# Layer 1's feed-forward part in one written order of block products and down products

## Chip, core and metric

The kernel runs on one core of one Trainium2 chip. A core has five engines with a queue each: TensorE (PE, with its weight loads shown as PEld), VectorE (DVE), ScalarE (ACT), GpSimd (POOL) and SyncE (SP), which here only issues DMAs. Each executes its queue in order and waits on semaphores for the others. The metric is device time in microseconds, the median of three runs.

## What is computed

A two-layer block over 1024 latent tokens of width 1024 and 256 context tokens. The change lies in the last part, the feed-forward of layer 1, which works on the latent tokens alone:

```python
x = x + g1 * o
h = _rms(x, norm2_g[i]) * (1.0 + sc2) + sh2
x = x + g2 * _swiglu(h, ffn_w_gate[i], ffn_w_up[i], ffn_w_down[i])

def _swiglu(h, wg, wu, wd):
    return (jax.nn.silu(h @ wg) * (h @ wu)) @ wd
```

The hidden width is 2816, which is 22 tiles of 128 (`NF = 22`). All values are 32-bit floats.

## The kernel before

**Precision.** A product of 32-bit floats is made of three matmuls: each operand is split into a rounded high part and a low part (the rest), and high by high, low by high and high by low are summed in PSUM (`mm3`, lines 74 to 76). The split of a weight tile is `parts_of` (lines 1236 to 1246): ScalarE casts to the high part (L1240), ScalarE copies that to a PSUM tile `pmisc` (L1244), and VectorE subtracts (L1245). With `G` as engine, Pool subtracts from SBUF directly. The ring for split weights has six places (`w_hi`, `w_lo`).

**Tiles of the feed-forward.** The tokens are done in two halves of 512 (`ci`). For each of 22 tiles (`f`) of the hidden width, gate and up together are a 2 x 2 block product, done as seven products of blocks instead of eight (`gate_up1`, with `product7`): each has 4 x 3 = 12 matmuls of 256 columns. Four raw weight blocks (b11, b12, b22, b21) of 128x512 are loaded by SP; four sums of them, t1 to t4, are made on Pool (L1328, L1329, L1343, L1347). The seven results are combined by VectorE (u2, u3, av, sg), with two Silu on ScalarE and two multiplications on VectorE (L1360, L1366), and the 512 values per partition of the tile's activation are split into `act_hi` (ScalarE, L1368) and `act_lo` (VectorE, L1369).

**Down.** Two tiles at a time are multiplied by w_down: eight down products (`down1`), each of 6 matmuls of 512 columns into one of three PSUM buffers `d_ps`, added into x by VectorE (L1394). The last eight of a half store x (L1396), issued from ScalarE's queue. The w_down weights are loaded by DMAs issued from Pool's queue (L1383) and split by ScalarE (L1384) and Pool (L1385).

**Norm and combine.** `norm1s` makes the normed activations of a half as a series of small steps, which other loops call for one at a time (`advance`). For the first half (`own0`) its steps run beside the output projection `out_proj1`; those of the second half (`own1`) begin beside the output projection too and go on with two steps per tile. The results of the second half are kept in DRAM (`h_d`) until the first half is done, then read back (`h_in`) and combined by `combine` into the 14 blocks `c_hi`, `c_lo` that the products read.

**Order of the work.** In this part the order in which each engine's queue is filled is the planner's: it takes the instructions as the program emits them and places them by its own estimates of cost. Other parts of the kernel fix the order of emission with `tc.manual_schedule`. In the program, a tile's seven products come one after the other, with the split of a product's weights just ahead of it (t1 and t2 of the first tile earlier), and after every second tile the eight down products of the pair before.

Of the kernel before, what the change touches and what calls it, by code (L numbers as in the profile page):

```python
# [16 lines left out]
P = 128  # L17
# [46 lines left out]
def build(tc, io):  # L64
# [1209 lines left out]
    def norm1s(ci, adder, done):  # L1274


        ts = slice(ci * 512, ci * 512 + 512)
        ss = wk.tile([P, 512], F32, name="nrm_ss")
        for i, k in enumerate(reversed(range(KT))):
            if i == 0:  # L1280
                S.activation(ss, x[:, k, ts], AF.Square)
            else:
                sq = wk.tile([P, 512], F32, name="nrm_sq", tag="t", bufs=4)
                S.activation(sq, x[:, k, ts], AF.Square)
                adder.tensor_tensor(ss, ss, sq, ALU.add)
            yield
        for r in norm_rstd(ss, 512, wk, ph):
            yield
        for i in range(4):
            both = []  # L1290
            for k in (i, i + 4):
                t = wk.tile([P, 512], F32, name="nrm_t", tag="t", bufs=4)
                V.scalar_tensor_tensor(t, x[:, k, ts], nA[3][:, k, 0:1], r, ALU.mult, ALU.mult)
                h = wk.tile([P, 512], F32, name="nrm_h", tag="wd", bufs=4)
                S.activation(h, t, AF.Identity, bias=vec(1, 3)[:, k, 0:1], scale=1.0)
                both.append(h)
                yield
            done(i, *both)
            yield
# [22 lines left out]
    def load_gate_up(f):  # L1322

        return [raw_half(io[w][1, f][:, i:i + 4]) for w, i in (("w_gate", 0), ("w_up", 0), ("w_up", 4), ("w_gate", 4))]

    def first_sums(b11, b12, b22):
        t1, t2 = (wk.tile([P, 4, P], F32, name=n, tag="t", bufs=4) for n in ("t1", "t2"))
        G.tensor_tensor(t1, b12, b11, ALU.subtract)  # L1328
        G.tensor_tensor(t2, b22, t1, ALU.subtract)  # L1329
        return t1, t2  # L1330

    def gate_up1(f, side=iter(()), raws=None):
        b11, b12, b22, b21 = raws[:4] if raws else load_gate_up(f)
        t1, t2 = raws[4:] if raws else first_sums(b11, b12, b22)
        t3, t4 = (wk.tile([P, 4, P], F32, name=n, tag="t", bufs=4) for n in ("t3", "t4"))
        p1, u2, u3, sg = (wk.tile([P, HT], F32, name=n) for n in ("p1", "u2", "u3", "sg"))
        av = wk.tile([P, 2, HT], F32, name="av", bufs=2)
        hi, lo = (wk.tile([P, 512], F32R, name=n, bufs=4) for n in ("act_hi", "act_lo"))
        w = parts_of(b11)
        ps = product7(w, 0)  # L1340
        S.copy(p1, ps)
        w = parts_of(t2)
        G.tensor_tensor(t3, b22, b12, ALU.subtract)  # L1343
        ps = product7(w, 4)
        V.tensor_tensor(u2, ps, p1, ALU.add)
        w = parts_of(t3)
        G.tensor_tensor(t4, t2, b21, ALU.subtract)  # L1347
        ps = product7(w, 5)
        V.tensor_tensor(u3, ps, u2, ALU.add)
        w = parts_of(t1)  # L1350
        ps = product7(w, 3)
        V.tensor_tensor(av[:, 1], ps, u3, ALU.add)
        V.tensor_tensor(u2, ps, u2, ALU.add)
        w = parts_of(t4)
        ps = product7(w, 2)
        V.tensor_tensor(u3, u3, ps, ALU.subtract)
        S.activation(u3, u3, AF.Silu)
        w = parts_of(b21)
        ps = product7(w, 1)
        V.tensor_tensor(av[:, 1], av[:, 1], u3, ALU.mult)  # L1360
        V.tensor_tensor(sg, ps, p1, ALU.add)
        S.activation(sg, sg, AF.Silu)
        w = parts_of(b22, G)
        ps = product7(w, 6)
        V.tensor_tensor(u2, ps, u2, ALU.add)
        V.tensor_tensor(av[:, 0], u2, sg, ALU.mult)  # L1366
        avf = av.rearrange("p a n -> p (a n)")
        S.copy(hi, avf)  # L1368
        V.tensor_tensor(lo, avf, fl(hi), ALU.subtract)  # L1369
        advance(side, 2)  # L1370
        return hi, lo
# [4 lines left out]
    h_d = tc.dram_tile([P, KT, 512], F32, name="h_d")  # L1376

    def down_weights1(f):

        w_in = w_room[f // 2 % 2]  # L1380
        for h in range(2):
            raw = wk.tile([P, 4, P], F32, name="wd_raw", tag="wd", bufs=4)
            G.dma_start(raw, io["w_down"][1, f][:, 4 * h:4 * h + 4])  # L1383
            S.copy(w_in[:, f % 2, h, 0], raw)  # L1384
            G.tensor_tensor(w_in[:, f % 2, h, 1], raw, fl(w_in[:, f % 2, h, 0]), ALU.subtract)  # L1385

    def down1(ci, fs, acts, last, amid=lambda dt: None):
        w_in = w_room[fs[0] // 2 % 2]
        ts = slice(ci * 512, ci * 512 + 512)
        for dt in range(KT):  # L1390
            ps = pd.tile([P, 512], F32, name="d_ps")
            for i in range(2):
                mm3(ps, w_in[:, i, dt // 4, 0, dt % 4], w_in[:, i, dt // 4, 1, dt % 4], *acts[i], i == 0, i == 1)
            V.scalar_tensor_tensor(x[:, dt, ts], ps, vec(1, 5)[:, dt, 0:1], x[:, dt, ts], ALU.mult, ALU.add)  # L1394
            if last:
                nc.scalar.dma_start(io["out"][:, dt, ts], x[:, dt, ts])  # L1396
            amid(dt)

    def keep(i, h0, h4):
        for k, h in ((i, h0), (i + 4, h4)):  # L1400
            nc.scalar.dma_start(h_d[:, k], h)

    own0 = norm1s(0, G, combine)
# [5 lines left out]
    own1 = norm1s(1, V, keep)  # L1409
    def first_tile():  # L1410
        raws = load_gate_up(0)
        return *raws, *first_sums(*raws[:3])

    ready = out_proj1(1, ready, own1, own0, then=first_tile)
    advance(own0, 99)
    for ci in range(2):
        acts = {}
        for f in range(NF):
            acts[f] = gate_up1(f, own1 if f else iter(()), ready if f + ci == 0 else None)
            down_weights1(f)  # L1420
            if f % 2 == 0 and 2 <= f < NF - 2:
                down1(ci, (f - 2, f - 1), [acts.pop(f - 2), acts.pop(f - 1)], False)

        h_in = []
        for i in range(4 if ci == 0 else 0):
            if i:
                h_in.append([raw_half(h_d[:, k]) for k in (i, i + 4)])
            else:
                h_in.append([wk.tile([P, 512], F32, name="h_in", tag=t) for t in ("nrm_ss", "nrm_r")])
                for h, k in zip(h_in[0], (0, 4)):  # L1430
                    nc.sync.dma_start(h, h_d[:, k])

        def amid(i):
            if h_in and i in (3, 7, 9, 12):
                combine(4 - len(h_in), *h_in.pop(0), tags=("t", "t"))

        for f in (NF - 4, NF - 2):
            down1(ci, (f, f + 1), [acts.pop(f), acts.pop(f + 1)], f == NF - 2,
                  lambda dt, f=f: amid(dt + (KT if f == NF - 2 else 0)))
# [113 lines left out]
```

## Time and profile before

| | us |
|---|---|
| median of three runs | 2944.4 |
| lowest and highest run | 2942.7, 2944.55 |
| the profiled execution | 2949.19 |
| its span on the core | 2947.4 |
| TensorE busy in the span | 2812.9 (95%) |
| VectorE, ScalarE, Pool busy | 1592.2, 1219.9, 799.0 |

The profile is one execution; its times are in microseconds from the start of the span, a duration in nanoseconds where it says "mean". A matmul's recorded time overlaps the next one's, so a busy TensorE can still lose time: the distance from one start to the next is what a matmul costs. In a row of the timeline, `[1.17 <-DVE x L1394]` says that the engine was idle 1.17 us before this instruction and that VectorE's instruction of line 1394 released it. In a row of groups, the figures after the bar are busy time, mean duration of one in ns, and the idle time ahead of them with what ended it. In a row of stretches stand the stretch, its length, busy time and count for each engine, the granted clock of TensorE as a share of full speed, and the DMA share and rate.

### The profile page before, as it was taken

What the parts mean: (1) busy time and instruction counts of PE and PEld (TensorE: products, weight loads), DVE (VectorE), ACT (ScalarE), POOL (GpSimd) and SP (SyncE); (2) the same over time, 40 slices, a digit from 0 to 9 for tenths busy, and PEclk for the clock granted to TensorE, in tenths of its full rate; (3) what the DMA queues carried; (4) which work ended last, traced back from release to release, by engine and by line L of the source; (5) the groups of instructions that cost most, each with busy time, mean ns of one, the idle gap of its engine ahead of it and who ended that gap; (6) DMA issues with size and microseconds to landing.
All of it is one profiled execution on the core that took longest, in us unless ns stands there. A gap on an engine that the chain in (4) does not pass through costs nothing. (4 is left out here: it accounts for less than half of the span.)

```text
span 2947.4 us, 44547 instructions
## 1 busy us (share of the span) xinstructions
PE 2812.9 (95%) x16874; PEld 2350.1 (80%) x16874; DVE 1592.2 (54%) x3144; ACT 1219.9 (41%) x2402; POOL 799.0 (27%) x870
## 2 busy tenths in 40 slices
PE   7989999999999999999989999999989899989999
PEld 5876768888888888888857778777768788888898
DVE  5775553633323333333575252566566777877776
ACT  4345552421111111111253231566447666666664
POOL 1122332000000000000130001455246666676662
PEclk9989999999999999999989999999999999999999
DMA  7236564211011110110124335876343322233231
GB/s 277 85 118 231 213 210 148 65 43 36 29 50 36 36 43 29 43 43 29 54 79 142 108 105 153 186 182 145 117 150 118 128 98 100 99 136 100 97 104 47
DMA packets 149349, 310.59 MB, mean 105 GB/s; under 512 B 13424, under 2 KB 71280, under 8 KB 142096
## 3 DMA queue, kind: packets, MB, share of 16 engines
q1 hardware_dynamic: 133664, 265.73, 28.9%
q0 software_dynamic: 8992, 31.40, 3.3%
q10 hardware_dynamic: 6480, 10.63, 1.0%
q8 instruction: 133, 2.18, 0.3%
q14 instruction: 80, 0.66, 0.1%
HBM read 264.58 MB, written 43.12 MB: 104 GB/s over the span
## 5 line engine op out<-in xcount | busy, mean ns | idle before, releaser
L74 PE MATMUL p_ps<-c_hi,w_hi 128*128 128x256 f32 x1232 | 344.6, 280 | 13.6 <-ACT w_hi L1240 4.6
L76 PE MATMUL p_ps<-c_hi,w_lo 128*128 128x256 f32 x1232 | 343.0, 279 | 4.5 <-DVE w_lo L1245 3.5
L75 PE MATMUL p_ps<-c_lo,w_hi 128*128 128x256 f32 x1232 | 342.7, 278 | 0.0
L810 POOL TENSOR_TENSOR nrm_ss<-nrm_ss,nrm_sq 128x512 f32<-128x512 f32 (+1 forms) x31 | 39.4, 1271 | 1012.9 <-PE d_ps L76 935.4
L775 ACT CAST w_hi<-w_raw 128x1024 fp32r<-128x1024 f32 x106 | 110.5, 1051 | 485.1 <-PE d_ps L75 270.4
L74 PEld LDWEIGHTS p_ps<-c_hi,w_hi 128*128 128x128 f32 x1232 | 233.7, 190 | 17.5 <-ACT w_hi L1240 6.6
L76 PEld LDWEIGHTS p_ps<-c_hi,w_lo 128*128 128x128 f32 x1232 | 233.5, 190 | 5.8 <-DVE w_lo L1245 4.5
L75 PEld LDWEIGHTS p_ps<-c_lo,w_hi 128*128 128x128 f32 x1232 | 233.6, 190 | 0.9
L580 POOL TENSOR_SCALAR pr<-pr,st 128x640 f32<-128x640 f32 (+2 forms) x208 | 156.9, 755 | 266.7 <-DVE st L579 176.8
L878 DVE SCALAR_TENSOR_TENSOR x<-d_ps,mod,x 128x512 f32<-128x512 f32 (+1 forms) x240 | 157.6, 661 | 125.2 <-PE d_ps L76 125.2
L776 DVE TENSOR_TENSOR w_lo<-w_raw,w_hi 128x1024 fp32r<-128x1024 f32 x102 | 124.1, 1224 | 184.0 <-ACT w_hi L775 181.6
L862 DVE TENSOR_TENSOR sg<-sg,u_ps 128x512 f32<-128x512 f32 (+1 forms) x66 | 39.6, 599 | 322.4 <-PE u_ps L76 322.4
L74 PE MATMUL d_ps<-act_hi,w_hi 128*128 128x512 f32 (+1 forms) x528 | 188.8, 358 | 3.5 <-DVE x L878 3.4
L75 PE MATMUL d_ps<-act_lo,w_hi 128*128 128x512 f32 (+1 forms) x528 | 188.7, 357 | 1.3 <-DVE act_lo L864 1.3
L75 PE MATMUL u_ps<-o_lo,w_hi 128*128 128x512 f32 (+1 forms) x528 | 189.3, 358 | 0.0
L76 PE MATMUL u_ps<-o_hi,w_lo 128*128 128x512 f32 (+1 forms) x528 | 189.1, 358 | 0.0
L74 PE MATMUL u_ps<-o_hi,w_hi 128*128 128x512 f32 (+1 forms) x528 | 189.0, 358 | 0.0
L76 PE MATMUL d_ps<-act_hi,w_lo 128*128 128x512 f32 (+1 forms) x528 | 188.9, 358 | 0.0
L74 PE MATMUL g_ps<-o_hi,w_hi 128*128 128x512 f32 (+1 forms) x528 | 188.2, 357 | 0.0
L75 PE MATMUL g_ps<-o_lo,w_hi 128*128 128x512 f32 (+1 forms) x528 | 188.2, 356 | 0.0
L76 PE MATMUL g_ps<-o_hi,w_lo 128*128 128x512 f32 (+1 forms) x528 | 188.2, 356 | 0.0
L574 ACT ACTIVATE pr<-sm,st 128x640 f32<-128x640 f32 (+4 forms) x208 | 162.9, 783 | 31.1 <-POOL sm L563 22.3
(329 smaller groups left out, 7494.6 us busy)
## 6 DMA issues: line engine op xcount, KB each, us to landing
ada_w<-ada_w SPq DMA_DIRECT2D x48, 1024.0 KB, 4.9
wd_raw<-w_down POOLq DMA_DIRECT2D x88, 256.0 KB, 2.9
w_raw<-w_gate SPq DMA_DIRECT2D x88, 256.0 KB, 2.6
w_raw<-w_up SPq DMA_DIRECT2D x88, 256.0 KB, 2.7
k<-k_d SPq DMA_DIRECT2D x28, 640.0 KB, 10.5
w_raw<-w_in SPq DMA_DIRECT2D x24, 512.0 KB, 4.0
w_raw<-w_gate SPq DMA_DIRECT2D x22, 512.0 KB, 3.5
w_raw<-w_up SPq DMA_DIRECT2D x22, 512.0 KB, 3.5
```

The costliest lines, as they stand in the source:

```text
L74: TE.matmul(out, lh, rh, start=first, stop=False)
L75: TE.matmul(out, lh, rl, start=False, stop=False)
L76: TE.matmul(out, ll, rh, start=False, stop=last)
L574: S.activation(self.pr[:, :n], self.sm[:, :n], AF.Exp, bias=st[:, 0:1], scale=-1.0, accum_out=st[:, 1:2])
L580: G.tensor_scalar(self.pr[:, :n], self.pr[:, :n], st[:, 3:4], 0.0, ALU.mult, ALU.add)
L775: S.copy(hi, raw)
L776: eng.tensor_tensor(lo, raw, fl(hi), ALU.subtract)
L810: adder(i).tensor_tensor(ss, ss, sq, ALU.add)
L862: V.tensor_tensor(sg[:, :n], sg[:, :n], u_ps[:, :n], ALU.mult)
L878: V.scalar_tensor_tensor(xs, self.shaped(ps[:, :n]), vec(l, 5)[:, dt, v:v + 1], xs, ALU.mult, ALU.add)
```

## The change

The whole part is emitted as one list of items: for each tile its seven products ("p"), after the third tile on also four down products ("d") of the pair before the last, and at the end of a half the last eight. A loop goes through the list inside `tc.manual_schedule`, so that TensorE, VectorE, ScalarE and Pool issue in the order of emission; SP's DMAs stay with the planner. Ahead of each item the loop emits the split of weights up to five products ahead (and at most seven items ahead), sums included. Steps that need a result of the item before (Silu, the multiplications, the split of the activation) are emitted one to three items later. In detail:

- `act_lo` is made on Pool instead of VectorE.
- The w_down loads are issued from SP instead of Pool, in the tile's fourth product; their split comes in the next tile.
- The second half's norm begins only in the second tile of the feed-forward, one step at every second product; its additions and multiplications are on Pool, with the scale moved into ScalarE's activation, its squares and its results in one buffer each (`nrm_r`, `nrm_ss`).
- Ahead of the first item, beside the last step of the output projection, five products' weights of the first tile are prepared instead of the two sums t1 and t2.
- `combine` for the second half stands at fixed places among the last twelve down products of the first half.

```diff
@@ -1271,7 +1271,7 @@
             advance(side, 3)
         return ready
-    def norm1s(ci, adder, done):
+    def norm1s(ci, done):
         ts = slice(ci * 512, ci * 512 + 512)
@@ -1280,23 +1280,31 @@
             if i == 0:
                 S.activation(ss, x[:, k, ts], AF.Square)
             else:
-                sq = wk.tile([P, 512], F32, name="nrm_sq", tag="t", bufs=4)
+                sq = wk.tile([P, 512], F32, name="nrm_sq", **(dict(tag="nrm_r") if ci else dict(tag="t", bufs=4)))
                 S.activation(sq, x[:, k, ts], AF.Square)
-                adder.tensor_tensor(ss, ss, sq, ALU.add)
+                G.tensor_tensor(ss, ss, sq, ALU.add)
             yield
         for r in norm_rstd(ss, 512, wk, ph):
             yield
         for i in range(4):
             both = []
             for k in (i, i + 4):
-                t = wk.tile([P, 512], F32, name="nrm_t", tag="t", bufs=4)
-                V.scalar_tensor_tensor(t, x[:, k, ts], nA[3][:, k, 0:1], r, ALU.mult, ALU.mult)
-                h = wk.tile([P, 512], F32, name="nrm_h", tag="wd", bufs=4)
-                S.activation(h, t, AF.Identity, bias=vec(1, 3)[:, k, 0:1], scale=1.0)
+                a, b = nA[3][:, k, 0:1], vec(1, 3)[:, k, 0:1]
+                if ci:
+                    h = wk.tile([P, 512], F32, name="nrm_h", tag="nrm_ss")
+                    G.tensor_tensor(h, x[:, k, ts], r, ALU.mult)
+                    S.activation(h, h, AF.Identity, bias=b, scale=a)
+                    nc.scalar.dma_start(h_d[:, k], h)
+                else:
+                    t = wk.tile([P, 512], F32, name="nrm_t", tag="t", bufs=4)
+                    V.scalar_tensor_tensor(t, x[:, k, ts], a, r, ALU.mult, ALU.mult)
+                    h = wk.tile([P, 512], F32, name="nrm_h", tag="wd", bufs=4)
+                    S.activation(h, t, AF.Identity, bias=b, scale=1.0)
                 both.append(h)
                 yield
-            done(i, *both)
-            yield
+            if not ci:
+                done(i, *both)
+                yield
     M1, M2 = slice(0, HT), slice(HT, 2 * HT)
@@ -1319,124 +1327,174 @@
             mm3(ps, w[0][:, k], w[1][:, k], c_hi[:, slot, k], c_lo[:, slot, k], k == 0, k == 3)
         return ps
-    def load_gate_up(f):
-
...
+    items = []
+    for ci in range(2):
+        for f in range(NF):
+            items += [("p", ci, f, s) for s in range(7)]
+            if f >= 2:
+                items += [("d", ci, f // 2 * 2 - 2, dt) for dt in range(f % 2 * 4, f % 2 * 4 + 4)]
+        items += [("d", ci, NF - 2, dt) for dt in range(KT)]
+    products = [(n, i) for n, i in enumerate(items) if i[0] == "p"]
+    LEAD_P, LEAD_I = 5, 7
+    tiles = {}
+    def load_tile(n):
+        if n < 2 * NF:
+            f = n % NF
+            tiles[n] = dict(b=[raw_half(io[w][1, f][:, i:i + 4])
+                               for w, i in (("w_gate", 0), ("w_up", 0), ("w_up", 4), ("w_gate", 4))], w={})
+    def prepare1(n, s):
+        if s == 0:
+            load_tile(n + 1)
+        d = tiles[n]
+        b11, b12, b22, b21 = d["b"]
+        def weight_sum(name, a, b):
+            d[name] = wk.tile([P, 4, P], F32, name=name, tag="t", bufs=4)
+            G.tensor_tensor(d[name], a, b, ALU.subtract)
+        if s == 0:
+            weight_sum("t1", b12, b11)
+            weight_sum("t2", b22, d["t1"])
+        elif s == 1:
+            weight_sum("t3", b22, b12)
+        elif s == 3:
+            weight_sum("t4", d["t2"], b21)
+        src = (b11, d["t2"], d.get("t3"), d["t1"], d.get("t4"), b21, b22)[s]
+        d["w"][s] = parts_of(src, G if s == 6 else V)
     w_room = [t.rearrange("p k n -> p (k n)").rearrange("p (f h t k n) -> p f h t k n", f=2, h=2, t=2, n=P)
               for t in h_out[1]]
     h_d = tc.dram_tile([P, KT, 512], F32, name="h_d")
-
-    def down_weights1(f):
-
-        w_in = w_room[f // 2 % 2]
+    down_raw = {}
+    def load_down(n):
         for h in range(2):
             raw = wk.tile([P, 4, P], F32, name="wd_raw", tag="wd", bufs=4)
-            G.dma_start(raw, io["w_down"][1, f][:, 4 * h:4 * h + 4])
-            S.copy(w_in[:, f % 2, h, 0], raw)
-            G.tensor_tensor(w_in[:, f % 2, h, 1], raw, fl(w_in[:, f % 2, h, 0]), ALU.subtract)
-
-    def down1(ci, fs, acts, last, amid=lambda dt: None):
-        w_in = w_room[fs[0] // 2 % 2]
+            nc.sync.dma_start(raw, io["w_down"][1, n % NF][:, 4 * h:4 * h + 4])
+            down_raw[n, h] = raw
+    def split_down(n, h):
+        f = n % NF
+        hi, lo = (w_room[f // 2 % 2][:, f % 2, h, t] for t in range(2))
+        raw = down_raw.pop((n, h))
+        S.copy(hi, raw)
+        G.tensor_tensor(lo, raw, fl(hi), ALU.subtract)
+    later = {}
+    def product(i, n, s):
+        d = tiles[n]
+        if s == 0:
+            for name in ("p1", "u2", "u3", "sg"):
+                d[name] = wk.tile([P, HT], F32, name=name)
+            d["av"] = wk.tile([P, 2, HT], F32, name="av", bufs=2)
+            d["act"] = [wk.tile([P, 512], F32R, name=m, bufs=4) for m in ("act_hi", "act_lo")]
+        p1, u2, u3, sg, av, (hi, lo) = (d[k] for k in ("p1", "u2", "u3", "sg", "av", "act"))
+        ps = product7(d["w"].pop(s), (0, 4, 5, 3, 2, 1, 6)[s])
+        def after(k, f):
+            later.setdefault(i + k, []).append(f)
+        if s == 0:
+            S.copy(p1, ps)
+        elif s == 1:
+            V.tensor_tensor(u2, ps, p1, ALU.add)
+        elif s == 2:
+            V.tensor_tensor(u3, ps, u2, ALU.add)
+        elif s == 3:
+            V.tensor_tensor(av[:, 1], ps, u3, ALU.add)
+            V.tensor_tensor(u2, ps, u2, ALU.add)
+        elif s == 4:
+            V.tensor_tensor(u3, u3, ps, ALU.subtract)
+            after(1, lambda: S.activation(u3, u3, AF.Silu))
+        elif s == 5:
+            V.tensor_tensor(sg, ps, p1, ALU.add)
+            after(1, lambda: S.activation(sg, sg, AF.Silu))
+            after(1, lambda: V.tensor_tensor(av[:, 1], av[:, 1], u3, ALU.mult))
+        else:
+            avf = av.rearrange("p a n -> p (a n)")
+            V.tensor_tensor(u2, ps, u2, ALU.add)
+            after(1, lambda: V.tensor_tensor(av[:, 0], u2, sg, ALU.mult))
+            after(2, lambda: S.copy(hi, avf))
+            after(3, lambda: G.tensor_tensor(lo, avf, fl(hi), ALU.subtract))
+    def down_product(ci, n, dt):
+        f = n % NF
+        w_in = w_room[f // 2 % 2]
         ts = slice(ci * 512, ci * 512 + 512)
-        for dt in range(KT):
-            ps = pd.tile([P, 512], F32, name="d_ps")
...
+        ps = pd.tile([P, 512], F32, name="d_ps")
+        for i in range(2):
+            mm3(ps, w_in[:, i, dt // 4, 0, dt % 4], w_in[:, i, dt // 4, 1, dt % 4], *tiles[n + i]["act"],
+                i == 0, i == 1)
+        V.scalar_tensor_tensor(x[:, dt, ts], ps, vec(1, 5)[:, dt, 0:1], x[:, dt, ts], ALU.mult, ALU.add)
+        if f == NF - 2:
+            nc.scalar.dma_start(io["out"][:, dt, ts], x[:, dt, ts])
+    own0 = norm1s(0, combine)
     ready = out_proj1(0, out_weights(KT - 1), own0, then=lambda: out_weights(KT - 1))
     pools.close(bg_cms[0])
     cc, cc_cm = pools.open("comb", side="right")
     c_hi = cc.tile([P, 7, 4, HT], F32R, name="c_hi")
     c_lo = cc.tile([P, 7, 4, HT], F32R, name="c_lo")
-    own1 = norm1s(1, V, keep)
+    own1 = norm1s(1, None)
     def first_tile():
-        raws = load_gate_up(0)
-        return *raws, *first_sums(*raws[:3])
-
-    ready = out_proj1(1, ready, own1, own0, then=first_tile)
+        load_tile(0)
+        for s in range(LEAD_P):
+            prepare1(0, s)
+    out_proj1(1, ready, iter(()), own0, then=first_tile)
     advance(own0, 99)
-    for ci in range(2):
-        acts = {}
...
+    done_p = LEAD_P
+    h_in = []
+    with tc.manual_schedule(engines={E.PE, E.DVE, E.Activation, E.Pool}):
+        now_p = 0
+        for i, (kind, ci, f, s) in enumerate(items):
+            n = ci * NF + f
+            while done_p < len(products) and done_p < now_p + LEAD_P + 1 and products[done_p][0] <= i + LEAD_I:
+                _, pc, pf, ps_ = products[done_p][1]
+                prepare1(pc * NF + pf, ps_)
+                done_p += 1
+            for step in later.pop(i, ()):
+                step()
+            if kind == "p":
+                product(i, n, s)
+                now_p += 1
+                if s == 3:
+                    load_down(n)
+                if f and s in (2, 5):
+                    split_down(n - 1, s // 5)
             else:
-                h_in.append([wk.tile([P, 512], F32, name="h_in", tag=t) for t in ("nrm_ss", "nrm_r")])
-                for h, k in zip(h_in[0], (0, 4)):
...
+                down_product(ci, n, s)
+                last = i + 12 >= len(items) or items[min(i + 12, len(items) - 1)][1] > ci
+                rest = sum(1 for it in items[i:i + 12] if it[0] == "d" and it[1] == ci) if last else 13
+                if last and rest in (12, 10):
+                    split_down(ci * NF + NF - 1, 0 if rest == 12 else 1)
+                if last and ci == 0 and rest in (11, 8, 5, 2):
+                    j = (11 - rest) // 3
+                    combine(j, *h_in[j], tags=("t", "t"))
+            if ci == 0 and kind == "p" and f and s % 2 == 0:
+                advance(own1, 1)
+            if ci == 0 and kind == "p" and f == NF - 1 and s == 6:
+                rooms = [dict(tag="nrm_ss"), dict(tag="nrm_r")], *([dict(tag="wd", bufs=4)] * 2,) * 3
+                for k, room in enumerate(rooms):
+                    h_in.append([raw_half(h_d[:, m]) if k in (1, 2) else wk.tile([P, 512], F32, name="h_in", **r)
+                                 for m, r in zip((k, k + 4), room)])
+                    if k in (0, 3):
+                        for h, m in zip(h_in[k], (k, k + 4)):
+                            nc.sync.dma_start(h, h_d[:, m])
+        for i in sorted(later):
+            for step in later[i]:
+                step()
     pools.close(ph_cm, pp_cm, pd_cm, wk_cm, ww_cm, wr_cm, xp_cm, cc_cm, bg_cms[1], cst_cm)
```

## What the change is predicted to do

> **What bounds the kernel now.** First the page's span, then layer 1's feed-forward part, which begins with the first product at 2204.3 us, in five stretches cut where a block of down products ends.
>
> ```profile
> span 2947.4 us, 44547 instructions
> ```
>
> The view by stretches, for the product tile p_ps and then for the down tile d_ps; columns: length, PE busy (matmuls), granted clock, DMA share, GB/s.
>
> ```profile
> 2204.30:2341.20 136.90, 76.02 (x588) 0.90 0.38 128
> 2341.20:2531.30 190.10, 115.30 (x1008) 1.00 0.30 100
> 2531.30:2638.50 107.20, 61.03 (x504) 0.98 0.36 123
> 2638.50:2892.40 253.90, 154.14 (x1344) 1.00 0.30 99
> 2892.40:2943.80 51.40, 28.74 (x252) 1.00 0.08 31
> ...
> 2204.30:2341.20 136.90, 40.45 (x145) 0.90 0.38 128
> 2341.20:2531.30 190.10, 69.68 (x289) 1.00 0.30 100
> 2531.30:2638.50 107.20, 35.22 (x145) 0.98 0.36 123
> 2638.50:2892.40 253.90, 92.84 (x385) 1.00 0.30 99
> 2892.40:2943.80 51.40, 22.79 (x98) 1.00 0.08 31
> ```
>
> A product is 12 matmuls, a down product 6 (one more at a cut is the neighbour's). So the stretches hold 49, 84, 42, 112, 21 products and 24, 48, 24, 64, 16 down products. The timeline gives what each costs when nothing waits:
>
> ```profile
> 2492.88 0.39 PE L75 MATMUL d_ps<-act_lo,h_lo 128*128 128x512 f32 x1
> ...
> 2499.41 0.39 PE L76 MATMUL d_ps<-act_hi,h_lo 128*128 128x512 f32 x1
> ...
> 2499.64 0.28 PE L74 MATMUL p_ps<-c_hi,w_hi 128*128 128x256 f32 x1
> ...
> 2504.75 0.28 PE L74 MATMUL p_ps<-c_hi,w_hi 128*128 128x256 f32 x1
> ```
>
> 28 down matmuls start in 6.53 us, so 1.40 us for a down product; 45 product matmuls in 5.11 us, so 1.363 us for a product. TensorE's need is 308 x 1.363 + 176 x 1.40 = 666 us of the 739.5. Lost by stretch: 136.9 - 100.4 = **36.5**, 190.1 - 181.7 = **8.4**, 107.2 - 90.9 = **16.3**, 253.9 - 242.3 = **11.6**, 51.4 - 51.0 = **0.4**: 73.2 us in all, the most that any order of these items can win here. Half lies in the first seven tiles. In the steady stretches 20 us are lost in 14 pairs of tiles, 1.4 us a pair, by one wait:
>
> ```profile
> 2488.87 1.30 POOL L1347 TENSOR_TENSOR t<-t,w_raw 128x512 f32<-128x512 f32 x1
> 2489.12 1.33 DVE L1366 TENSOR_TENSOR av<-u,sg 128x256 f32<-128x256 f32 x1
> 2490.37 0.67 DVE L1245 TENSOR_TENSOR w_lo<-w_raw,pmisc 128x512 fp32r<-128x512 f32 x1
> ...
> 2491.14 0.69 DVE L1369 TENSOR_TENSOR act_lo<-av,act_hi 128x512 fp32r<-128x512 f32 x1
> 2491.75 2.06 DVE L1394 SCALAR_TENSOR_TENSOR x<-d_ps,mod,x 128x512 f32<-128x512 f32 x3
> ...
> 2492.54 0.50 PE L74 MATMUL d_ps<-act_hi,h_lo 128*128 128x512 f32 x1 [1.17 <-DVE x L1394]
> ```
>
> VectorE reaches the first x late, the three PSUM buffers of d_ps are full, TensorE waits. So the bound is TensorE, and what it loses is set by how late VectorE's queue comes to x.
>
> **The change part by part.** No matmul goes or comes. What changes is four queues, now as written. Their prices:
>
> ```profile
> L1244 ACT COPY pmisc<-w_hi 128x512 f32<-128x512 f32 x264 | 155.2, 590 | 11.6 <-DVE w_lo L1245 4.8
> L1240 ACT CAST w_hi<-t 128x512 fp32r<-128x512 f32 x176 | 107.9, 618 | 18.7 <-POOL t L1329 6.2 <-PE p_ps L75 4.6 <-POOL t L1343 3.9
> L1341 ACT COPY p<-p_ps 128x256 f32<-128x256 f32 x44 | 16.1, 366 | 0.0
> ...
> L1329 POOL TENSOR_TENSOR t<-w_raw,t 128x512 f32<-128x512 f32 x44 | 58.0, 1319 | 8.7 <-issue 3.6 <-DVE c_lo L1314 1.6 <-POOL t L1328 0.2
> L1385 POOL TENSOR_TENSOR h_lo<-wd_raw,h_lo 128x512 fp32r<-128x512 f32 x40 | 51.7, 1294 | 41.4 <-ACT h_lo L1384 41.0
> L1383 POOL DMA_DIRECT2D wd_raw<-w_down x87 | 48.1, 554 | 18.1 <-POOL h_lo L1385 6.2 <-POOL h_hi L1385 5.6 <-PE p_ps L76 4.2
> ...
> L1394 DVE SCALAR_TENSOR_TENSOR x<-d_ps,mod,x 128x512 f32<-128x512 f32 x176 | 128.6, 747 | 62.4 <-PE d_ps L76 62.4
> L1245 DVE TENSOR_TENSOR w_lo<-t,pmisc 128x512 fp32r<-128x512 f32 x176 | 120.2, 684 | 36.0 <-ACT pmisc L1244 34.1 <-POOL w_lo L1245 0.8
> L1366 DVE TENSOR_TENSOR av<-u,sg 128x256 f32<-128x256 f32 x44 | 50.4, 1145 | 4.1
> L1365 DVE TENSOR_TENSOR u<-p_ps,u 128x256 f32<-128x256 f32 x44 | 18.3, 415 | 1.7 <-PE p_ps L76 1.7
> ```
>
> **Steady tile (seven products, four down products, 15.15 us of TensorE).** Loads by engine: VectorE 6 w_lo, 7 of 0.42, two av, 4 x, about 12 us; ScalarE 6 pmisc, 7 casts, p, two Silu, three more casts, about 11; Pool four sums, w_lo, two w_down parts and now act_lo, 8 x 1.3 = 10.4 (the 554 ns DMA issues go to SP, which has time). None is full; what counts is the order. I walk one tile, in us after product 0 starts, a queue's next instruction starting when its own engine and its inputs are free. Product 0 is out at 1.5: ScalarE's p 1.6-2.0, then the cast of product 6's weights, for which a ring of six leaves no room earlier, 1.9-2.5, a w_down cast to 3.0. Pool follows: w_lo 2.6-3.9, w_down part to 5.1, t1 to 6.4, t2 to 7.7, t3 to 9.0. Next product 1's weights: cast of t2 and pmisc to 9.0, VectorE's w_lo 9.1-9.7. On ScalarE Silu and a w_down cast stand before the cast of t3, so pmisc ends at 11.0 and VectorE's w_lo at 11.7. Behind it, av: Pool is in t4 (11.2-12.5), so av runs 12.5-12.9; then u, one more w_lo to 13.8, av to 14.2, and only now x of the first down product, to 14.8. The fourth down product needs that buffer at 7 x 1.363 + 3 x 1.40 = 13.74. It waits **1.1 us, in every tile**, where before it was 1.4 in two. What was queued behind act_lo is now queued behind the weights of five products ahead: w_lo waits for pmisc, that for Pool's sums, and x stands behind it. Bounds: 0.3 (no port wait, shorter hand-overs) to 1.5 (Pool a tenth slower). I take 1.1. 30 such tiles (12, 16 and 2 in the second, fourth and fifth stretch): 33 for 20.4 us, **+12.6**.
>
> **The port.** L1366 (both inputs in SBUF) takes 1145 ns, L1365 with the same shape but one input in PSUM 415. At 2489.12 it ran to 2490.45, just past the end of Pool's t4 at 2490.17: it waits for Pool's current instruction. One row shows worse:
>
> ```profile
> 2325.34 7.60 DVE L1369 TENSOR_TENSOR act_lo<-av,act_hi 128x512 fp32r<-128x512 f32 x1
> ```
>
> It waited through six of Pool's instructions. The change takes L1369 off VectorE, but leaves both av there and fuller runs on Pool. The Trainium skill, "SBUF — State Buffer", section "Who interferes with whom", says that a DVE instruction with two SBUF inputs and a GpSimd instruction that reads SBUF exclude each other, the later one blocking until the first is done; by that rule the steady term stays as walked, by the 7.60 us row it can be several us more in a tile; the rows of L1366 agree with the rule, the 7.60 does not.
>
> **First seven tiles.** The second half's norm leaves VectorE: seven adds and eight multiplications on Pool (1.3 each, 19.5 us) in tiles 1 to 5, four steps a tile, each with a ScalarE instruction before or behind it, the squares in a single buffer (ScalarE waits for Pool's add) and so the results (Pool waits for the store).
>
> ```profile
> h_d<-nrm_h ACTq DMA_DIRECT2D x8, 256.0 KB, 2.3
> ```
>
> Pool in tile 1: 11 x 1.3 = 14.3 us for 9.5 of TensorE: 4.8 lost. Tile 0 about 4 (sums of its last weights and of tile 1's). In tiles 2 to 4 the walk gets 1.1 + two norm instructions ahead of t2 (2.6) + one between t3 and t4 (1.3) + their ScalarE instructions and store issues (1.9) + a store's landing (about 1): 7.9 each; tile 5 half, tile 6 1.1: sum 38. Waits as long cost clock:
>
> ```profile
> 2330.00:2340.00 10.00, 6.33 (x19) 0.66 0.49 157
> ```
>
> A wait of about 7 us before it left this slice at 0.66, while the 1.17 us waits left 1.00: I add 5. So 43 for 36.5, **+6.5**; bounds 26 (Pool's excess alone) and 58. The page "TensorE: Matmul & The Clock Gate" of the Trainium skill, Part 1, puts the half clock after an idle window of about 3.4 us; the rows agree.
>
> **The turn to the second half.** The last eight down products of the first half store x from ScalarE:
>
> ```profile
> 2579.47 0.34 ACTq L1396 DMA_DIRECT2D out<-x  x1
> ```
>
> In written order ScalarE cannot pass this issue, which waits for VectorE's x; behind it stand cast and pmisc (1.2) of the next half's weights, behind them w_lo (0.65), behind that the next x (0.7): 2.9 us round where a down product takes 1.4. Six weights fall there, 9 us, less two buffers (2.8); VectorE's sixteen c_lo make 12 down products cost it 22 us against 16.8; then tiles 22 to 24 start with Pool behind. I take 28 (bounds 14 and 38) for 16.3: **+11.7**.
>
> **Before the first product.** The norm's steps beside the output projection go, weights of five products come. Two waits there can go:
>
> ```profile
> 2190.29 0.50 PE L76 MATMUL d_ps<-h_hi,w_lo 128*128 128x512 f32 x1 [1.58 <-DVE w_lo L1245]
> ...
> 2196.31 0.50 PE L76 MATMUL d_ps<-h_hi,w_lo 128*128 128x512 f32 x1 [2.96 <-DVE w_lo L1245]
> ```
>
> **-4.5** (bounds -6 and 0). Sum: 12.6 + 6.5 + 11.7 - 4.5 = +26.3 us.
>
> **Rivals.** (1) Faster: the lead suffices. If x of the first down product ends 1.1 us sooner, by 13.7 us after product 0, the steady wait is nil; if the lead of five also swallows the norm (20 left) and the turn costs 14, 34 us are lost for 73.2: -39 - 4.5, about 2901. For it: no engine is over 80% in the steady tile. Against: the walk's chain from t2 to x. From 77.7 us lost upwards the kernel is slower; it decides at the fourth down product. (2) No port wait: av finds Pool idle, 0.5 a tile, -18 of the sum: 2953. Against: L1366's 1145. (3) Starved: av waits through a run of Pool's, as at 2325.34, in five tiles at about 6 us: 3001. For: longer runs; against: 1145 ns as the mean of 44 leaves no room for many waits of 7 us. (4) It doesn't do what it says: SP keeps its own order, so loads can land late whatever is written.
>
> ```profile
> w_raw<-w_gate SPq DMA_DIRECT2D x88, 256.0 KB, 2.6
> ```
>
> A load has most of a tile of 15 us for its 2.6, so I give it nothing.
>
> **How the numbers follow.** Forecast 0.48, (1) 0.22, (2) 0.20, (3) 0.10. The profiled execution takes 2949.2, 4.8 above the median of 2944.4; the difference carries over: 2944.4 + 26.3 = 2971. Bounds summed: 9 + 26 + 14 - 6 = 43 lost, -30; 45 + 58 + 38 = 141, +68. Cut at both ends, with part of (1) and (3) outside: 2908 to 3008. A change under 0.2% (5.9 us) can't be told from none: slower 0.66 (forecast, (3), 0.08 of (2)), same 0.08, faster 0.26.
>
> **What would show it.** Right: a wait of d_ps for x at the fourth down product of nearly every tile, about 1 us; VectorE's gap before w_lo released by pmisc, that of ScalarE by Pool's t; the largest waits in tiles 2 to 4 and at the turn; no wait in the output projection. Wrong: steady tiles of 15.2 us, or Pool with idle time in tiles 1 to 5; then the order hides what I queue up, and the kernel is faster.

## The result, and the profile after

The changed kernel takes **2989.45 us** (median of four runs, 2985.47 to 2993.26) where the kernel before takes 2944.48 (four runs): 45.0 us more, a ratio of 1.0153 with a 95% interval of 1.0136 to 1.0171. The profiled execution took 2990.69 us, 41.5 more than that of before.

The feed-forward part now begins at 2198.3 us. These are the stretches of the kernel after, cut where tiles 7, 19 and 25 begin and where the last down product starts and has run its 1.40 us; first for p_ps, then for d_ps, columns as before.

```profile
2198.30:2346.20 147.90, 76.70 (x588) 0.88 0.30 100
2346.20:2541.00 194.80, 116.35 (x1008) 1.00 0.30 98
2541.00:2665.20 124.20, 62.41 (x505) 0.94 0.31 107
2665.20:2984.90 319.70, 185.61 (x1596) 1.00 0.27 90
...
2198.30:2346.20 147.90, 33.88 (x121) 0.88 0.30 100
2346.20:2541.00 194.80, 72.13 (x289) 1.00 0.30 98
2541.00:2665.20 124.20, 39.42 (x145) 0.94 0.31 107
2665.20:2984.90 319.70, 125.14 (x505) 1.00 0.27 90
```

They hold 49, 84, 42, 133 products and 20, 48, 24, 84 down products, which need 94.8, 181.7, 90.8 and 298.9 us. Lost are **53.1, 13.1, 33.4 and 20.8**, together 120.4 for 73.2. TensorE's busy time is nearly as it was; it waits more. Two rows of the page after say where (its chain of work that ended last, its group of VectorE's w_lo):

```profile
PE 14%; POOL 6%; ACT 5%; issue 5%; DVE 5%; DMA 2%; ACTq 0%; POOLq 0%; DVEq 0%
POOL t L1359 3%; PE po L1170 2%; ACT w_hi L1240 2%; DMA w_raw<-w_gate 2%; PE d_ps L74 2%; PE pt_ps L589 2%; PE s_ps L599 1%; PE d_ps L75 1%; PE d_ps L76 1%; POOL w_lo L1245 1%; DVE av L1421 1%; DVE x L1437 1%; DVE w_lo L1245 1%; ACT pmisc L1244 1%; PE s_ps L600 1%
...
L1245 DVE TENSOR_TENSOR w_lo<-t,pmisc 128x512 fp32r<-128x512 f32 x176 | 119.7, 680 | 150.8 <-ACT pmisc L1244 145.3
```

The shares of the chain add to 37% of the span, so far back it could be followed; among its lines the sums t on Pool come first. VectorE's idle time before w_lo, 36.0 us before, is 150.8. The view of waits in the feed-forward part names one wait far ahead of the others:

```profile
PE d_ps L74 <- DVE x L1437: 66.0, 43, 8.1
PE p_ps L74 <- DVE u L1414: 7.3, 4, 3.0
```

43 waits for x (total, times, longest). A steady tile of the kernel after, from the timelines of its engines, shows why:

```profile
2442.13 0.50 PE L74 MATMUL d_ps<-act_hi,h_lo 128*128 128x512 f32 x1 [0.85 <-DVE x L1437]
2442.14 1.30 POOL L1427 TENSOR_TENSOR act_lo<-av,act_hi 128x512 fp32r<-128x512 f32 x1 [2.27 <-ACT act_hi L1426]
...
2445.20 0.37 ACT L1407 COPY p<-p_ps 128x256 f32<-128x256 f32 x1 [1.99 <-PE p_ps L76]
2445.47 0.62 ACT L1240 CAST w_hi<-w_raw 128x512 fp32r<-128x512 f32 x1
...
2446.17 1.29 POOL L1245 TENSOR_TENSOR w_lo<-w_raw,w_hi 128x512 fp32r<-128x512 f32 x1 [2.73 <-ACT w_hi L1240]
2447.43 1.28 POOL L1388 TENSOR_TENSOR h_hi<-wd_raw,h_hi 128x512 fp32r<-128x512 f32 x1
2448.68 1.28 POOL L1359 TENSOR_TENSOR t<-w_raw 128x512 f32<-128x512 f32 x1
2450.04 1.30 POOL L1359 TENSOR_TENSOR t<-w_raw,t 128x512 f32<-128x512 f32 x1
...
2451.37 0.62 ACT L1240 CAST w_hi<-t 128x512 fp32r<-128x512 f32 x1 [3.62 <-POOL t L1359]
...
2452.72 0.69 DVE L1245 TENSOR_TENSOR w_lo<-t,pmisc 128x512 fp32r<-128x512 f32 x1 [1.65 <-ACT pmisc L1244]
...
2454.72 0.69 DVE L1245 TENSOR_TENSOR w_lo<-t,pmisc 128x512 fp32r<-128x512 f32 x1 [0.98 <-ACT pmisc L1244]
2455.33 1.06 DVE L1421 TENSOR_TENSOR av<-av,u 128x256 f32<-128x256 f32 x1
...
2457.57 0.74 DVE L1437 SCALAR_TENSOR_TENSOR x<-d_ps,mod,x 128x512 f32<-128x512 f32 x1
...
2458.36 0.51 PE L74 MATMUL d_ps<-act_hi,h_lo 128*128 128x512 f32 x1 [0.85 <-DVE x L1437]
```

Read it downwards: ScalarE must copy p (a result of product 0) before it casts product 6's weights; Pool stands idle 2.73 us for that cast, because its w_lo is next in the written order; the sums t1 and t2 stand behind it; ScalarE idles 3.62 us for t2; VectorE 1.65 us for pmisc, and again 0.98; its x starts only at 2457.57; and the fourth down product comes late by a wait that repeats every 16.23 us (2442.13, 2458.36), where a tile needs 15.15.

### The profile page after: what moved, and what is told of

Same layout as the page of the kernel before. It is cut to its first block, busy times and chain, and to the rows that moved or that the text cites. A ratio compares the mean times of both kernels' runs of the same rounds, so it can differ in the third digit from the quotient of the medians.

```text
span 2988.9 us, 44472 instructions
## 1 busy us (share of the span) xinstructions
PE 2821.1 (94%) x16874; PEld 2352.6 (79%) x16874; DVE 1515.3 (51%) x3085; ACT 1212.9 (41%) x2402; POOL 810.4 (27%) x841
## 5 line engine op out<-in xcount | busy, mean ns | idle before, releaser
L1245 DVE TENSOR_TENSOR w_lo<-t,pmisc 128x512 fp32r<-128x512 f32 x176 | 119.7, 680 | 150.8 <-ACT pmisc L1244 145.3
## 6 DMA issues: line engine op xcount, KB each, us to landing
k<-k_d SPq DMA_DIRECT2D x28, 640.0 KB, 10.3
```

Source lines behind the costliest of these rows:

```text
L1245: eng.tensor_tensor(lo, src, first, ALU.subtract)
```

## The experiments

Each kernel is the changed one with one edit, unless it says otherwise. For the expectations the walk of one tile in the prediction was carried through all items: a queue's next instruction starts when its engine, its inputs and its buffers are free, with the trace's durations. This walk knows no half clock (behind a long wait the matmuls start about twice as far apart as usual for some us); for the order as changed it gives 107 us lost (the trace: 120.4). "Lost" is as above, by the same four stretches.

| kernel | median us | ratio to before, 95% interval | lost: tiles 0-6, 7-18, 19-24, 25-43 | all |
|---|---|---|---|---|
| before (its own stretches) | 2944.5 | 1 | 36.5, 8.4, 16.3, 12.0 | 73.2 |
| as changed | 2989.45 | 1.0153 [1.0136, 1.0171] | 53.1, 13.1, 33.4, 20.8 | 120.4 |
| e1_sums_ahead | 2936.26 | 0.9973 [0.9963, 0.9982] | 45.4, 0, 20.8, 0 | 65 |
| e2_x_first | 2975.58 | 1.0110 [1.0092, 1.0129] | 48.6, 8.3, 33.7, 13.3 | 104 |
| e3_out_sp | 2981.21 | 1.0132 [1.0117, 1.0147] | 55.3, 13.1, 22.9, 20.8 | 112 |
| e4_norm_vector | 2987.63 | 1.0155 [1.0136, 1.0174] | 48.7, 13.1, 33.3, 19.9 | 115 |
| e6_actlo_vector | 2989.61 | 1.0161 [1.0146, 1.0176] | 52.5, 13.1, 30.1, 19.6 | 115 |
| e7_no_order | 2925.53 | 0.9946 [0.9930, 0.9963] | 30.1, 6.6, 5.5, 9.5 | 52 |
| e8_all | 2891.57 | 0.9825 [0.9811, 0.9840] | 7.5, 3.7, 11.2, 0 | 22 |
| e9_norm_one | 2991.19 | 1.0162 [1.0147, 1.0178] | 29.7, 36.7, 32.1, 19.6 | 118 |
| e10_all_no_order | 2921.52 | 0.9918 [0.9895, 0.9941] | 18.6, 9.7, 9.8, 10.3 | 48 |
| e11_lead4 | 3046.36 | 1.0340 [1.0317, 1.0364] | 59.9, 29.9, 36.6, 46.6 | 173 |
| e12_lead4_sums | 2941.93 | 0.9984 [0.9973, 0.9996] | 50.5, 0, 21.0, 0 | 71 |

### The steady wait: where the sums stand

`first_sums` makes t1 and t2 of a tile; at `s == 6` it now stands ahead of product 6's split.

```diff
-        if s == 0:
-            weight_sum("t1", b12, b11)
-            weight_sum("t2", b22, d["t1"])
+        if s == 0 and n == 0:
+            first_sums(d)
...
+        elif s == 6 and n + 1 in tiles:
+            first_sums(tiles[n + 1])
```

> Only the place of two sums changes: t1 and t2 of the next tile stand ahead of the split of product 6's weights on Pool, instead of behind it. Theory A (the written order: Pool waits for ScalarE's cast of product 6's weights with nothing to do, then t1 and t2 come late, so pmisc, w_lo and the x behind it): the wait at the fourth down product goes in all steady tiles (30 us of it), and the turn loses some 8 us less; the queue walk with the trace's durations gives 60 us lost for its 107 with the order as changed, so -47 us: about 2942 us. Theory B (Pool has too much work, 8 x 1.3 us in a tile): Pool's work is the same, the time too, 2985 to 2993 us. Theory C (x waits behind w_lo whatever Pool does): no change in the steady tiles.

The timeline of e1_sums_ahead, a steady tile whose first product starts at 2443.11 (that of the tile shown above at 2443.63):

```profile
2441.28 1.30 POOL L1433 TENSOR_TENSOR act_lo<-av,act_hi 128x512 fp32r<-128x512 f32 x1 [2.27 <-ACT act_hi L1432]
2442.54 1.30 POOL L1359 TENSOR_TENSOR t<-w_raw 128x512 f32<-128x512 f32 x1
2443.92 1.29 POOL L1359 TENSOR_TENSOR t<-w_raw,t 128x512 f32<-128x512 f32 x1
...
2445.65 1.29 POOL L1245 TENSOR_TENSOR w_lo<-w_raw,w_hi 128x512 fp32r<-128x512 f32 x1 [0.44 <-ACT w_hi L1240]
...
2447.34 0.62 ACT L1240 CAST w_hi<-t 128x512 fp32r<-128x512 f32 x1
...
2453.36 1.05 DVE L1427 TENSOR_TENSOR av<-av,u 128x256 f32<-128x256 f32 x1
```

The two sums fill the gap in which Pool waited (2.73 us became 0.44), t2's cast starts 4.2 us after the tile's first product instead of 7.7, and no steady tile loses anything. Two lines moved give 53 us back, 12.6 of them at the turn (8 were expected there), and the kernel is below before. With the same eight Pool instructions in a tile, Pool's load (theory B) can't be the cause, and x standing behind w_lo (C) isn't by itself. The last row is of use for rival (2): av still takes 1.05 us, where with Pool idle it takes 0.41, and it costs nothing here.

```diff
-                down_product(ci, n, s)
+                down_product(ci, n, s)
+                ahead()
```

`ahead` is the loop that prepares the weights; ahead of the item it now stands only for products.

> In the items of down products the weights ahead are prepared behind the item, so VectorE has x before the next w_lo. Theory A (order): the walk gives 85 us lost for 107, the wait at the fourth down product falls from 1.0 to 0.6 us in a steady tile and the turn hardly changes: -22 us, about 2967 us. Theory B (Pool's load): no change, 2985 to 2993. Theory C (x behind w_lo is all of it): the steady wait goes entirely, -30 us.

x ahead of w_lo helps by 14 us, less than I thought: 0.7 us stay in a steady tile (the walk: 0.6).

```diff
-            after(3, lambda: G.tensor_tensor(lo, avf, fl(hi), ALU.subtract))
+            after(3, lambda: V.tensor_tensor(lo, avf, fl(hi), ALU.subtract))
```

> act_lo goes back from Pool to VectorE, at its place in the written order. Theory A: Pool is idle before and behind act_lo in the steady tile, so taking it away frees nothing that anyone waits for: the walk gives -3.5 us (first tiles and turn), the steady wait stays at 1.1: about 2986 us. Theory B (Pool's load sets the steady wait): 1.3 us less on Pool in each tile, the wait goes: about 2957 us. Port rival: act_lo has two inputs in SBUF and waits through runs of Pool's: slower than 2993 us.

Nothing in the median, where 2986 was expected: some 5 us less are lost, but in that profile the first product begins 3.1 us later. The steady wait stays, and Pool's load falls a second time as its cause. Nor did the port rival come; the view by source line of e6_actlo_vector has the shortest, median and longest of act_lo's 44 in ns:

```profile
L1427 DVE TENSOR_TENSOR act_lo<-av,act_hi x44: 680/685/1747, 2224.7 to 2970.0; 128x512 fp32r<-128x512 f32 x44
```

Two runs change the lead itself:

```diff
-    LEAD_P, LEAD_I = 5, 7
+    LEAD_P, LEAD_I = 4, 7
```

> Weights four products ahead instead of five, nothing else. Theory A: the chain from product 6's cast over t1 and t2 to w_lo begins one product later against x, so the wait at the fourth down product doubles: the walk gives 2.2 us in a steady tile for 1.1 and 149 us lost for 107, +42: about 3031 us. Rival (fewer weights stand ahead of x in VectorE's queue, so x comes sooner): faster than 2985 us. Rival (Pool's load): no change in the steady tiles.

> Weights four products ahead and t1 and t2 ahead of product 6's weights on Pool. Theory A: with the sums out of the chain the lead of four is enough; the walk gives 59.8 us lost, as with five (60.2): about 2936 us, no steady wait. Rival (a lead of four is too short by itself): the 42 us of the shorter lead come on top, 2960 us or more.

A lead shorter by one product doubles the steady wait (the view of waits of e11_lead4):

```profile
PE d_ps L74 <- DVE x L1437: 107.5, 43, 8.6
```

and alone costs 57 us; beside the moved sums it can't be told from a lead of five (the intervals of e1 and e12 overlap), and no steady tile waits. The fifth product of lead only made up for part of the chain.

### The first seven tiles: the second half's norm

```diff
-                G.tensor_tensor(ss, ss, sq, ALU.add)
+                (V if ci else G).tensor_tensor(ss, ss, sq, ALU.add)
...
-                    G.tensor_tensor(h, x[:, k, ts], r, ALU.mult)
+                    V.tensor_tensor(h, x[:, k, ts], r, ALU.mult)
```

> The seven adds and eight multiplications of the second half's norm go from Pool to VectorE, at the same places of the order. Theory B (Pool's excess in tiles 1 to 5, the 4.8 us a tile of my prediction): Pool is rid of 19.5 us, the first seven tiles lose 15 to 20 us less: about 2972 us. Theory A' (not Pool's time but the queues' coupling: the squares' and the results' single buffers and the store hold up ScalarE and whoever adds): the walk gives 1 us: about 2988 us.

Taking all of the norm's Pool work away brings 2 us in the median (the intervals overlap) and 4.4 in that stretch, 2.7 of them in tile 2. The groups of the kernel after in its first seven tiles (2198.3 to 2346.2) show what Pool and ScalarE waited for.

```profile
L1240 ACT CAST w_hi<-t 128x512 fp32r<-128x512 f32 x32 | 19.7, 615 | 21.9 <-POOL t L1359 20.3 <-ACT nrm_h L1296 1.6
...
L1296 ACT ACTIVATE nrm_h<-nrm_h,mod,nA 128x512 f32<-128x512 f32 x8 | 6.5, 816 | 14.2 <-POOL nrm_h L1295 14.2
```

```profile
L1245 POOL TENSOR_TENSOR w_lo<-w_raw,w_hi 128x512 fp32r<-128x512 f32 x7 | 9.0, 1291 | 31.9 <-ACT w_hi L1240 31.9
L1427 POOL TENSOR_TENSOR act_lo<-av,act_hi 128x512 fp32r<-128x512 f32 x7 | 9.0, 1290 | 12.2 <-ACT act_hi L1426 12.2
```

ScalarE waits 14.2 us for Pool's norm multiplications, with the casts behind; Pool waits 31.9 us for product 6's cast, with the sums behind. Two queues in written order hold up each other by turns. Yet Pool is busy only 90.26 us of these 147.9 (the stretch with all engines, in the order PE, PEld, DVE, ACT, POOL):

```profile
2198.30:2346.20 147.90, 110.36 (x725) 100.81 (x724) 71.13 (x135) 92.61 (x165) 90.26 (x72) 0.88 0.30 100
```

The tiles differ: Pool is busy 9.4 of 16.1 us in tile 1, but 20.8 of 26.1 in tile 2, where five of the norm's seven additions stand. There Pool's time counts; e4_norm_vector took 7.2 us of it away, and the tile still loses 8.3 us for 11.0.

Without the norm's work Pool has still more room and waits still longer, in e4_norm_vector's first seven tiles for the same cast:

```profile
L1245 POOL TENSOR_TENSOR w_lo<-w_raw,w_hi 128x512 fp32r<-128x512 f32 x7 | 9.1, 1306 | 38.4 <-ACT w_hi L1240 38.4
```

One norm step a tile:

```diff
-            if ci == 0 and kind == "p" and f and s % 2 == 0:
+            if ci == 0 and kind == "p" and f and s == 0:
```

> The second half's norm takes one step in a tile (at its first product) in place of four, nothing else. Theory A' (each step stands in the queue ahead of t2's chain, however few there are): the walk moves the loss and hardly lessens it, first seven tiles 24 for 41, tiles 7 to 18 29 for 13, in all -2 us (the half clock of the longest waits goes besides, up to -10): 2978 to 2988 us. Theory B (Pool's excess over TensorE in tiles 1 to 5): with one step a tile Pool has 9 x 1.3 = 11.7 us of work for 15.2 of TensorE, so the excess goes: -15 us or more on top of the clock, below 2970 us, and tiles 7 to 18 stay at 1.1 us each.

The loss moves and stays: 23 us less in the first stretch, 24 more in the second. A tile with a result step loses 2.3 us instead of 1.1, and the timeline of e9_norm_one shows the 1.2:

```profile
2494.49 0.37 ACT L1407 COPY p<-p_ps 128x256 f32<-128x256 f32 x1 [1.98 <-PE p_ps L76]
2494.76 0.82 ACT L1296 ACTIVATE nrm_h<-nrm_h,mod,nA 128x512 f32<-128x512 f32 x1
2495.61 0.33 ACTq L1297 DMA_DIRECT2D h_d<-nrm_h  x1
2495.97 0.62 ACT L1240 CAST w_hi<-w_raw 128x512 fp32r<-128x512 f32 x1 [0.40 <-ACT nrm_h L1296]
...
2496.67 1.30 POOL L1245 TENSOR_TENSOR w_lo<-w_raw,w_hi 128x512 fp32r<-128x512 f32 x1 [2.69 <-ACT w_hi L1240]
```

The step and its store stand between p and product 6's cast, the head of the chain to t2. The time is 3 us above the expected range: the half clock did not go but moved with the waits (by the count given further down, 9.3 us in the first stretch of the kernel as changed, here about 7 in the first and 6 in the second).

### The turn

```diff
-            nc.scalar.dma_start(io["out"][:, dt, ts], x[:, dt, ts])
+            nc.sync.dma_start(io["out"][:, dt, ts], x[:, dt, ts])
```

> The stores of x at the end of a half are issued from SP instead of ScalarE. If the ring through ScalarE's queue (issue waits for x, cast and pmisc behind it, w_lo, next x) costs what I put on it at the turn, the turn (between the last tiles of the first half and the third of the second) loses 9 us less by the walk: about 2980 us, nothing elsewhere. Rival: the turn is bound by Pool and by combine's work: 2985 to 2993 us.

8.2 us in the median, 10.5 in its stretch and nothing in the steady ones: the ring is there. In the kernel after it shows in ScalarE's timeline: of the seven distances between the eight store issues three are 3.11 us and one 3.03, where TensorE needs a down product's 1.40; with casts of `combine` between them the other three are 3.93 to 6.48.

```profile
2600.40 0.34 ACTq L1439 DMA_DIRECT2D out<-x  x1
2600.79 0.62 ACT L1240 CAST w_hi<-t 128x512 fp32r<-128x512 f32 x1 [3.37 <-DVE x L1437]
2601.44 0.59 ACT L1244 COPY pmisc<-w_hi 128x512 f32<-128x512 f32 x1
2603.51 0.34 ACTq L1439 DMA_DIRECT2D out<-x  x1
```

The ring is not all of the turn. e3_out_sp gains in tiles 21, the last of the first half, and 22 (11.5 us lost for 21.8). e1_sums_ahead, with the stores still on ScalarE, gains 12.6 us in the same stretch, nearly all in tiles 22 to 24 (8.1 for 17.9).

### The order as a whole

The same emission, with the planner filling the queues:

```diff
-    with tc.manual_schedule(engines={E.PE, E.DVE, E.Activation, E.Pool}):
+    if True:
```

> The same items, emitted in the same sequence, but without the written order: the planner fills the queues of TensorE, VectorE, ScalarE and Pool by its own costs, as before. Theory A (the loss is in the order of the queues, not in the work that was moved): it comes near the kernel before, 2930 to 2955 us, and the wait at the fourth down product is gone or at another place. Rival (the work moved to Pool costs, in whatever order): 2975 to 2995 us.

Better than expected: 18 us below the before of its own series (2943.27), 64 below the written order, with TensorE's items in the very same sequence. So the list of items and the work moved with it are a gain when the planner orders them; the way the other queues were written out is the loss. The last two runs bring the edits of e1, e3, e4 and e9 together, with t3 one split earlier, once in written order and once under the planner:

```diff
-        elif s == 1:
-            weight_sum("t3", b22, b12)
+        if s == 0:
+            weight_sum(d, "t3", b22, b12)
```

> Three orders mended at once: t1 and t2 of the next tile ahead of product 6's weights on Pool (and t3 with the first split), the stores of x from SP, and the norm at one step a tile with its adds and multiplications on VectorE. Theory A: the queue walk gives 20 us lost for its 107 (8 in the first seven tiles, 10 at the turn, none in the steady tiles), and waits this short cost no clock, so some -90 to -97 us against the kernel as changed: 2893 to 2900 us, below both kernels. Rival (port: av and the norm's instructions on VectorE wait through runs of Pool's): 2910 us or more, with rows of several us among av's.

> The three mended orders of e8_all, emitted in the same sequence, but with the planner filling the four queues. e8_all had 22 us lost, the changed items under the planner 52, of which 13 in tile 0 and 0.6 in each steady tile. If the planner chooses well whatever it is given: it gains from the spread norm too, 2895 to 2910 us. If its steady order (0.6 us a tile) and its tile 0 stay: 22 us from tiles 1 to 6 and the turn at most, 2905 to 2925 us, above e8_all. I expect the second.

e8_all takes 2891.57 us, 97.9 less than the kernel as changed and 51.7 less than before in the same series, and is the fastest of all; the walk had 2893 to 2900. Its view of waits in the feed-forward part:

```profile
PE d_ps L74 <- DVE x L1443: 6.6, 4, 2.3
```

Of 43 waits for x four are left, of 66.0 us 6.6. Tried one at a time, the four edits give 53.2 (e1), 8.2 (e3), 1.8 (e4) and -1.7 us (e9), together 61.5; in e8_all they give 97.9. They depend on each other: tiles 2 to 5 lose 38.3 us as changed, 36.7 with the sums ahead alone, 15.4 with one norm step a tile alone, and 1.5 in e8_all, and the steps that cost 24 us in tiles 7 to 18 of e9_norm_one leave 3.7 there. How the other 36 us divide among the pairs of edits, and what t3's place does, was not tried. Under the planner the three mended places bring little (the intervals of e7 and e10 overlap): it keeps 0.6 us in a steady tile, and 13 in tile 0.

## Why the prediction was nearly right

The sign and the cause in the steady tiles were right, and the time lies inside the range; the effect was 45 us where the text has 26. By its steps:

- **Steady tile, right.** The walk gave 1.1 us at the fourth down product of every tile; the trace has 1.1 by the period. The stretches with the 30 such tiles lose 33.9 (13.1 + 20.8), forecast 33, so +13.5 against 20.4. The chain is the one walked (p, product 6's cast, Pool, t2, pmisc, w_lo, x): e1_sums_ahead cuts it and the wait is gone, e11_lead4 shortens the lead and it doubles. In the tile shown, counted from its first product, Pool's w_lo starts at 2.5 us (walked 2.6), t2's cast at 7.7 (7.7), the w_lo behind it at 9.1 (9.1), and x ends at 14.7 (14.8). What share of the 1.1 the port has was not tried by itself; the av at 2455.33 took 1.06 us where the shortest took 0.42, so some 0.6 us, an estimate.
- **First seven tiles, mis-sized, and for a wrong reason in part.** 53.1 lost where I had 43: this is the step that failed, +16.6 for +6.5. I built it on Pool's excess ("11 x 1.3 = 14.3 us for 9.5 of TensorE") with queue waits added from tile 2 on. In tile 1, of which this was said, Pool is busy 9.4 us and idle 6.7, and it is idle in the tiles behind too, which the text names as a sign that it is wrong and the kernel faster; the kernel was slower all the same, since Pool was idle behind ScalarE's cast. By tile the loss is 7.2, 6.6, 11.0, 12.4, 10.1, 4.8 and 1.1 where the text has 4, 4.8, three times 7.9, half of that and 1.1 (and 5 of clock for all): every tile up to the sixth was put too low, tiles 2 to 4 are the worst as it says. e4_norm_vector shows that Pool's time is the smaller part, e9_norm_one that fewer steps a tile only move the loss while t2's chain stands as it is. That each step costs by its place in ScalarE's queue is argued from the timelines; no run moved a step alone. About 4 of the 10 us missing are clock: 80 distances between matmuls in that stretch are about twice the usual and make 9.3 us, for which I had added 5. Before has 59 such distances and 7.7 us in its own first seven tiles, so of the +16.6 the clock is only 1.6; the rest is waiting.
- **The turn, mechanism right, one cause and the clock left out.** 33.4 lost, forecast 28, so +17.1 for +11.7. The ring takes 3.11 us (forecast 2.9) and e3_out_sp has it at 8 to 10 us. That moving the sums takes 12.6 us off the turn shows that t2's chain holds it up as well; the text has only "tiles 22 to 24 start with Pool behind", without a price. In the same count 38 doubled distances make 4.9 us, for which I had put nothing; the turn of before has about 2.1 us of them, so the clock makes 2.8 of the +17.1. The stretch's granted clock of 0.94, before 0.98, agrees.
- **Before the first product, right in sign by the profiles, not settled in size.** -6.0 in the two profiles, forecast -4.5. The waits of the output projection for w_lo fell from 4.5 to 0.9 us, which gives 3.6. But kernels with the same instructions up to there began their first product between 2193.5 (e2_x_first) and 2202.4 us (e9_norm_one), all ahead of the 2204.3 of before, of which there is one profile.

Sum: 13.5 + 16.6 + 17.1 - 6.0 = 41.2, which is the difference of the profiled executions (41.5); the text's sum assumed that it carries over to the medians, which lie 45.0 apart. One slip in the range: the lower sum, 30 us less, gives 2914 and the range begins at 2908, so that end was moved outwards where the text says inwards; the result lies towards the other end and isn't touched by it.

**Rivals.** (1) "The lead suffices": it doesn't, as emitted. What the rival describes, no steady wait and a kernel below before, came when the sums stood ahead, with a lead of four as with five. (2) No port wait: the 0.5 a tile didn't come; e1_sums_ahead shows that the port wait of av remains and is harmless once w_lo is early. (3) Starved: no; in the view by source line of the kernel after the two av (shortest, median, longest in ns) never took longer than one wait for one Pool instruction makes them:

```profile
L1421 DVE TENSOR_TENSOR av<-av,u x44: 418/1057/1332, 2217.6 to 2967.3; 128x256 f32<-128x256 f32 x44
...
L1425 DVE TENSOR_TENSOR av<-u,sg x44: 408/411/1143, 2219.0 to 2969.1; 128x256 f32<-128x256 f32 x44
```

By the Trainium skill, "SBUF — State Buffer", section "Who interferes with whom", the later one blocks until the first instruction is done: these 88 agree with that, as one Pool instruction takes 1.3 us, and so do the 44 of act_lo in e6_actlo_vector. The 7.60 us row of before has no companion here, and what made it was not tried. (4) SP's own order: no load stood in the chain that e1_sums_ahead cut.

## What to carry to other kernels

When an order is written out by hand, each engine's queue has to be walked for the instruction that waits longest, and independent work (here two sums, ready for 2.7 us) belongs ahead of it, not behind: Pool and ScalarE, at some 60% load in the first seven tiles, lost more to each other's order than their load explains. A longer lead hides such a chain only in part; look for the chain before adding lead. Nothing of low urgency (a norm step, a store that waits for x) should stand in the queue ahead of what the next weights need.

## What the runs showed of the hardware

The half clock was a larger part of the loss than I had put: in the two stretches with long waits 9.3 and 4.9 us, estimated from the doubled distances above; but before has 7.7 and about 2.1, so it is a small part of what the change added. In the kernel after, the timeline has a wait of 7.35 us that ends at 2254.58, behind it down matmuls 0.43 us apart (0.23 where nothing waits), and the slice around it (p_ps alone) a granted clock of 0.66:

```profile
2254.58 0.80 PE L74 MATMUL d_ps<-act_hi,h_hi 128*128 128x512 f32 x1 [7.35 <-DVE x L1437]
...
2255.60 0.63 PE L76 MATMUL d_ps<-act_hi,h_hi 128*128 128x512 f32 x1
2256.03 0.63 PE L74 MATMUL d_ps<-act_hi,h_hi 128*128 128x512 f32 x1
```

```profile
2250.00:2260.00 10.00, 2.17 (x12) 0.66 0.24 75
```

e8_all, whose longest wait for x is 2.3 us, has a granted clock of 0.98 in its first seven tiles and loses 1.9 us by the same count.
